# A two-block model kernel on one Trainium2 core: layer 0's modulation rows at another place, and the short convolution's input read from SBUF

## The chip, the cores and the metric

One core of one Trainium2 chip. The metric is device time in microseconds (us) of one execution, smaller is better; PE is TensorE (matrix products), PEld its weight load, DVE is VectorE, ACT ScalarE, POOL GpSimd, SP SyncE, whose queue here issues nearly all loads and stores.

## The reference

A first block (a Hyena long convolution and an HGRN2 scan side by side as mixer, then a mixture of 16 experts that pick their tokens) is followed by a second block of two layers of attention with Fourier and pooling branches. The parts that the change touches:

```python
def short_conv(u, w, b, n_rows):          # first block, width 3, along grid rows of 64
    up = jnp.pad(u.reshape(bn, n_rows, row_len, C), ((0, 0), (0, 0), (pad, pad), (0, 0)))
    y = b + sum(up[:, :, j:j + row_len] * w[j] for j in range(HY_SHORT))

def hyena_mixer(p, n_rows, conv_w, conv_b, filt, bias):
    u = short_conv(p, conv_w, conv_b, n_rows)
    v, x1, x2 = jnp.split(u, 3, axis=-1)
    z = x1 * long_conv(v, hf[:, 0], bias[0])
    y = x2 * long_conv(z, hf[:, 1], bias[1])

def second_block(x, c, ctx, c_ctx, norm_g, w_mod, b_mod, ...):
    for l in range(DEPTH_2):              # 2 layers
        x, ctx = mixer_layer(l, x, ctx, c, c_ctx, norm_g[l], w_mod[l], b_mod[l], ...)
```

Each layer of the second block scales, shifts and gates its input by modulation vectors silu(c) @ w_mod[l] + b_mod[l], for the tokens and, from c_ctx, for the context: 1024 x 3072 weights a layer. The first block has its own (ada_w, 1024 x 6144). x is 1024 tokens of 1024 values, the context 256 tokens, all float32.

## The kernel before

The program runs in stages. 0 to about 110 us: constants, the first two of six column groups of the first block's modulation, normed tokens. To 776.5 us, the **Hyena stage**: the long convolution's filters, spectra and products (`filter_time`, `filter_spectra`, `hyena`) beside the projections of the tokens (`hy_proj`, `hg_proj`) and beside `mods_layer(0, ...)`, the second block's modulation for layer 0. To 1041 us, the **HGRN scans**: `ctx_state` and four times `hgrn_head`, with small work of the first block's remaining modulation (`mods_tail`) and of the second block's context (`ctx_first`, `ctx_side`) woven in. To about 1203 us, **out_proj** and the routing. Then the experts, to about 2600 us, and the two attention layers.

Each engine runs its instructions in one fixed order. The program is written as streams; `side_by_side` (lines 1979 to 1990) weighs those of the Hyena stage against one another, and a scheduler, which sees the whole program, then sets the order on each engine by the rings of buffers that are open (`K.open`, with the count of each ring) and its own estimate of times. PE works in order, and `self.dma` (line 160) puts every load and store on SP's one queue.

Names and lines that matter here:
- `mod_rows` (290 to 313) makes 1024 modulation columns for both c and c_ctx. There are eight **k-steps**: the load of 128 x 1024 weights (512 KB), and two matmuls (L193) that hold the weights as the moving operand and the two silu columns as the stationary one, 2 x 512 each. Then come two bias loads, four adds on DVE (L171), two stores. The whole of `mods_layer` (333 to 343) is three such groups, 24 k-steps, then `rows_to_cols` (315), which reads the rows back and transposes them, and two instructions that make the scale A. `mods_tail` (345) is four groups, 32 k-steps.
- `hy_proj` (789 to 832): for each of 12 channel tiles and 2 token halves, `proj` (421) makes 128 x 512 of projection in a PSUM buffer `pp` (three of them) by 24 matmuls (L188 to L190). The short convolution (821 to 828) is one ACT instruction (scale and bias, middle tap) into a `u2` buffer `u`, and two DVE instructions (L180) that add the left and right tap, all three reading `pp`. `turn` transposes the previous result, copies it out (L168) and stores it.
- `run` (1993): pools at 1996 to 2004, `side_by_side` at 2007 to 2009, the scans' extra work at 2022 to 2030 (PSUM buffers `cp` and `cm`, one each; weight rings `wr` of two and `mr` of one).
- `ctx_first` transposes the normed context (`cp<-ident,cx`), applies layer 0's scale and shift (`cu`, and `Tc`, its two split halves), and projects it: the matmuls `cp<-Tc,wh` and `cp<-Tc,wl`, in blocks of 24. `ctx_side` makes its side branches and its gate by more such blocks. They need layer 0's modulation.

```python
side_by_side((30, 450, [(K.filter_time(), 2.4), (K.filter_spectra(), 2.1), (K.hyena(), 5)]),
           (0, 64, [(K.hy_proj(), 1), (K.hg_proj(), 1)]),
           (0, 4, [(K.mods_layer(0, "mp", "u2", ("mr",), False), 1)]))
```

Of the kernel before, what the change touches and what calls it, by code (L numbers as in the profile page):

```python
# [14 lines left out]
AF = mybir.ActivationFunctionType  # L15
# [99 lines left out]
class Work:  # L115
# [673 lines left out]
    def hy_proj(self):  # L789

        I = self.I
        w = I["w_in"][0]
        ocw, ocb = self.offs["hy_conv_w"], self.offs["hy_conv_b"]
        self.dhy = self.dram([3, 2, 2, 128, 4, 256], name="dhy")
        cw2 = self.cst([128, 4, 4], name="cw2")

        def turn(u, dst):
            pt = self.ps("pp", [128, 4, 128])
            for a in range(4):
                self.tr(pt[:, a], u[:, a * 128:a * 128 + 128])  # L800
            ut = self.t("u2", [128, 4, 128])
            self.cp(ut, pt)
            self.dma(dst, ut)

        late = None
        for g in range(3):
            if g == 2:
                yield from self.hg_values()
                for j in range(3):
                    self.tt(cw2[:, j], self.ca[:, ocw + j * 12 + 8:ocw + j * 12 + 12], self.finv, MUL)  # L810
                self.tt(cw2[:, 3], self.ca[:, ocb + 8:ocb + 12], self.finv, MUL)
            for half in range(2):
                for ct in range(2):
                    c = g * 4 + half * 2 + ct
                    wp = self.wunits(w, c * 128, 128, self.nc.gpsimd)
                    if g == 2:
                        cw = [cw2[:, j, c - 8:c - 7] for j in range(4)]
                    else:
                        cw = [self.ca[:, ocw + j * 12 + c:ocw + j * 12 + c + 1] for j in range(3)] + [self.ca[:, ocb + c:ocb + c + 1]]
                    for th in range(2):  # L820
                        ps = self.proj(wp, self.hT, th * 512, 512, "pp")
                        u = self.t("u2")
                        self.act(u, ps, AF.Identity, scale=cw[1], bias=cw[3])
                        pv = ps.rearrange("p (r c) -> p r c", c=64)
                        uv = u.rearrange("p (r c) -> p r c", c=64)
                        self.stt(uv[:, :, 1:], pv[:, :, :63], cw[0], uv[:, :, 1:], MUL, ADD)
                        self.stt(uv[:, :, :63], pv[:, :, 1:], cw[2], uv[:, :, :63], MUL, ADD)
                        if late:
                            turn(*late)
                        late = (u, self.dhy[g, half, th][:, :, ct * 128:ct * 128 + 128])  # L830
                        yield
        turn(*late)
# [1146 lines left out]
def side_by_side(*streams):  # L1979

    todo = [[-lead / total, total, list(gens)] for lead, total, gens in streams]
    while todo:
        s = min(todo, key=lambda t: t[0])
        g, w = s[2][0]
        if next(g, todo) is todo:
            s[2].pop(0)
            if not s[2]:
                todo.remove(s)
        else:
            s[0] += w / s[1]  # L1990


def run(K):
    fst = ExitStack()
    with ExitStack() as e1:
        K.open(e1, "left", ar=3, ah=4, al=4)
        K.open_ps(e1, "left", pp=3, mp=1)
        K.open(e1, "left", u2=4, T=16)
        K.open_ps(fst, "right", pf=4)
        K.open(fst, "right", f4=7, fb=5)  # L2000
        with ExitStack() as e2:
            K.open(e2, "right", cr=6, x=4, c=2, mr=4)
            K.start()
        K.open(fst, "right", y=3, t=4, H=2, hs=3, dc=2, ri=7, ra=2, mr=1)
        K.load_dft()
        K.mods_first()
        side_by_side((30, 450, [(K.filter_time(), 2.4), (K.filter_spectra(), 2.1), (K.hyena(), 5)]),
                   (0, 64, [(K.hy_proj(), 1), (K.hg_proj(), 1)]),
                   (0, 4, [(K.mods_layer(0, "mp", "u2", ("mr",), False), 1)]))
    fst.close()  # L2010
    with ExitStack() as cx:
        with ExitStack() as e1:
            K.open_ps(e1, "left", ph0=3, ph1=3)
            K.open(e1, "left", hmk=1, hS=2)
            for p in "01":
                K.open(e1, "left", **{"hi" + p: 6, "hw" + p: 5, "h2" + p: 3, "hm" + p: 4, "hT1" + p: 2, "hT2" + p: 4})
            K.ctx_state()
            for h in range(4):
                K.hgrn_head(h)
            K.open(cx, "right", wr=2, wh=2, wl=2, cu=6, cv=2, Tc=4, lg=2)  # L2020
            K.pfx = "c"
            with ExitStack() as e2:
                K.open_ps(e2, "right", cp=1, cm=1)
                K.open(e2, "right", mr=1)
                for _ in K.mods_tail("cm", "cv", ("wr", "wr", "mr"), False):
                    pass
                K.ctx_first()
                K.ctx_side()
                for _ in K.mods_layer(1, "cm", "cv", ("wr", "wr", "mr"), False):
                    pass  # L2030
        K.open_ps(cx, "right", cp=1, cm=1)
        K.pfx = "o"
        em = cx.enter_context(ExitStack())
        with ExitStack() as e0:
            K.open_ps(e0, "left", pp=3, pq=2, pi=1)
            with ExitStack() as e1:
                K.open(e1, "left", xm=3, rw=1, wo=16, m4=3, yt=6, u2=3)
                K.out_proj()
            K.open(em, "left", el=4, eh=4, er=10)
            with ExitStack() as e1:  # L2040
                K.open(e1, "left", twr=3, twh=3, twl=3)
                K.open(e1, "left", aff=1, tk=12, tp=2, af=4)
                K.topk()
                K.pfx = "c"
                K.ctx_heads("tw")
        with ExitStack() as e1:
            K.open_ps(e1, "left", et=1, ea=3, ey=2)
            K.open(e1, "right", g2b=1, xg=1, xf=1, xh=4, sa=4, hh=4, yo=2)
            side_by_side((0, 64, [(K.moe(), 1)]), (CL, CT, [(K.ctx_rest(), 1)]))
    K.pfx = ""  # L2050
    with ExitStack() as e1, ExitStack() as e0, ExitStack() as ec:
        K.open(e0, "right", T0=16)
        rope = K.lat_pools(ec)
        hT = K.first_rows()
        K.lat_path(hT, rope, ec, e0, e1)


class Kern:
# [9 lines left out]
    def start(self):  # L2068
        W = self.work
        W.pc, W.psm, W.pd, W.one = self.pc, self.psm, self.pd, self.one  # L2070
        run(W)
# [119 lines left out]
```

## Time and profile before

| what | value |
|---|---|
| median of 3 runs (lowest, highest) | 3840.05 us (3839.73, 3846.28) |
| the profiled execution's own time | 3841.8 us |
| its span, first to last instruction | 3839.7 us |
| mean granted TensorE clock | 0.963 of 2.4 GHz |
| PE, DVE, ACT, POOL busy | 92%, 71%, 58%, 29% of the span |
| DMA | 780.49 MB, mean 203 GB/s |

The shares are means over stages with different limits; the table of stretches below tells them apart. A row of that table gives, for one stretch of the span, the busy time of each engine with its number of instructions, the granted clock as a share of full speed, and the busy share and rate of the DMA engines. A row on a group of instructions gives line, engine, operation, output and inputs (buffer numbers left out), shape and number; then busy time, mean duration in ns, and the idle time of the engine ahead of them with what ended it. A matmul of float32 with 512 columns shows as two records.

### The profile page before, as it was taken

The page shows a single profiled execution, that of the slowest core. Times are in us where ns is not written, and L with a number is a line of the kernel's source. Part 1 is how long each engine was busy: PE and PEld are TensorE (multiplying, and loading weights), DVE is VectorE, ACT ScalarE, POOL GpSimd, SP SyncE. Part 2 cuts the span into 40 slices and gives each one's busy share as a digit, 9 for nine tenths or more (in the row PEclk, how much of TensorE's full clock was granted, in tenths as well). Part 3 has the DMA queues.
Part 4 walks back from the last instruction along what each step waited for, and adds up shares of the span by engine and source line. Part 5 has one row for each costly group of instructions (what it writes and reads, how often), then busy time and mean ns, then how long its engine had stood idle before and what let it go on. Part 6 is the DMA issues. An engine that isn't in the chain of part 4 may idle for free. (4 is left out here: it accounts for less than half of the span.)

```text
span 3839.7 us, 50939 instructions
## 1 busy us (share of the span) xinstructions
PE 3533.6 (92%) x17554; PEld 2841.9 (74%) x17554; DVE 2727.8 (71%) x4143; ACT 2219.1 (58%) x3568; POOL 1127.8 (29%) x702
## 2 busy tenths in 40 slices
PE   5998999968897799999999999979999899999989
PEld 2666878747867678787777777768777688877767
DVE  3488667777735789889889889866666744576672
ACT  4432322354525786787777777755576754456762
POOL 2355423364414214112112111001333610133361
PEclk9999999979998899999999999989999999999999
DMA  6765444464476699999999999952311144131133
GB/s 206 220 222 181 130 145 128 141 211 147 132 246 218 200 341 347 336 333 364 371 366 358 370 367 357 364 185 81 128 60 43 47 155 132 59 128 54 39 104 115
DMA packets 503019, 780.49 MB, mean 203 GB/s; under 512 B 35025, under 2 KB 238823, under 8 KB 502504
## 3 DMA queue, kind: packets, MB, share of 16 engines
q1 hardware_dynamic: 496136, 755.74, 57.8%
q0 software_dynamic: 5600, 20.43, 2.0%
q8 instruction: 138, 2.26, 0.2%
q10 hardware_dynamic: 1024, 1.06, 0.1%
q14 instruction: 121, 0.99, 0.1%
HBM read 669.00 MB, written 107.05 MB: 202 GB/s over the span
## 5 line engine op out<-in xcount | busy, mean ns | idle before, releaser
L171 DVE TENSOR_TENSOR el<-er,eh 128x1024 fp32r<-128x1024 f32 x763 | 950.7, 1296 | 107.9 <-ACT eh L168 105.8
L168 ACT ACTIVATE eh<-er 128x1024 fp32r<-128x1024 f32 x768 | 782.4, 1057 | 116.1 <-PE ea L190 83.5
L189 PE MATMUL ea<-el,xh 128*128 128x512 f32 x1024 | 413.9, 404 | 21.0 <-DVE el L171 18.1
L188 PE MATMUL ea<-eh,xh 128*128 128x512 f32 x1024 | 399.2, 393 | 2.4 <-ACT eh L168 2.2
L190 PE MATMUL ea<-eh,xh 128*128 128x512 f32 x1024 | 401.1, 392 | 0.0
L1265 POOL DMA_INDIRECT acc<-yo,idx x16 | 74.0, 4626 | 808.8 <-DVE yo L180 754.9
L1488 DVE TENSOR_SCALAR_CACHE_REDUCE E<-s,rq 128x512 f32<-128x512 f32 (+1 forms) x384 | 237.2, 656 | 80.8 <-PE s L193 70.0
L189 PEld LDWEIGHTS ea<-el,xh 128*128 128x128 f32 x1024 | 192.6, 188 | 94.1 <-DVE el L171 58.4
L165 ACT ACTIVATE E<-E,a 128x1280 f32<-128x1280 f32 x160 | 216.7, 1359 | 66.5 <-DVE a L1492 61.5
L193 PE MATMUL s<-KA,QA 128*128 128x512 f32 (+1 forms) x768 | 212.6, 398 | 32.1 <-DVE E L1488 31.1
L188 PEld LDWEIGHTS ea<-eh,xh 128*128 128x128 f32 x1024 | 192.5, 188 | 46.4 <-ACT eh L168 4.2
L190 PEld LDWEIGHTS ea<-eh,xh 128*128 128x128 f32 x1024 | 193.0, 189 | 34.3 <-POOL xh L171 0.3
L189 PE MATMUL ey<-el,hh 128*128 128x512 f32 x512 | 203.8, 398 | 6.2 <-DVE el L171 6.2
L188 PE MATMUL ey<-eh,hh 128*128 128x512 f32 x512 | 202.0, 399 | 2.1 <-ACT eh L168 2.1
L190 PE MATMUL ey<-eh,hh 128*128 128x512 f32 x512 | 200.3, 391 | 0.0
L171 POOL TENSOR_TENSOR wl<-wr,wh 128x1024 fp32r<-128x1024 f32 (+1 forms) x48 | 116.6, 2434 | 253.7 <-ACT wh L168 193.3
L193 PEld LDWEIGHTS s<-KA,QA 128*128 128x128 f32 x768 | 131.4, 199 | 78.8 <-DVE E L1488 60.3
L168 ACT ACTIVATE u<-pp 32x512 f32<-32x512 f32 (+2 forms) x212 | 124.4, 587 | 106.3 <-PE pp L190 85.6
L193 PE MATMUL po<-th,V 128*128 128x256 f32 x640 | 172.5, 395 | 13.7 <-ACT th L168 13.6
L188 PE MATMUL pp<-T,ah 128*128 128x512 f32 x448 | 183.0, 408 | 1.6 <-ACT ah L168 1.6
L190 PE MATMUL pp<-T,al 128*128 128x512 f32 x448 | 179.2, 400 | 0.4 <-POOL al L171 0.4
L189 PE MATMUL pp<-T,ah 128*128 128x512 f32 x448 | 178.7, 399 | 0.0
(516 smaller groups left out, 8944.2 us busy)
## 6 DMA issues: line engine op xcount, KB each, us to landing
er<-in_exp_w_dram SPq DMA_DIRECT2D x768, 512.0 KB
wr<-in_w_in_dram SPq DMA_DIRECT2D x60, 512.0 KB
ar<-in_w_in_dram SPq DMA_DIRECT2D x64, 256.0 KB
mr<-in_w_mod_dram SPq DMA_DIRECT2D x30, 512.0 KB
wr<-in_ada_w_dram SPq DMA_DIRECT2D x24, 512.0 KB
wr<-in_w_out_dram SPq DMA_DIRECT2D x24, 512.0 KB
Hd<-hs SPq DMA_DIRECT2D x72, 128.0 KB
H<-Hd SPq DMA_DIRECT2D x36, 256.0 KB
```

The costliest lines, as they stand in the source:

```text
L165: return self.nc.scalar.activation(out, in_, func, **kw)
L168: return self.nc.scalar.activation(out, in_, AF.Copy)
L171: return (eng or self.nc.vector).tensor_tensor(out, a, b, op=op)
L188: mm(out, lh, rh, start=first, stop=False)
L189: mm(out, lh, rl, start=False, stop=False)
L190: mm(out, ll, rh, start=False, stop=last)
L193: self.nc.tensor.matmul(out, l, r, start=first, stop=last)
L1265: nc.gpsimd.indirect_dma_start(out=self.acc, out_offset=x[0], in_=yo, in_offset=None, compute_op=ADD)
L1488: nc.vector.tensor_scalar(E[:, k0:k1], o, r, None, op0=MUL, op1=ALU.min, accum_out=mx[:, m, j:j + 1] if nc_ > 1 else mc)
```

## The change

Three edits. (a) In the short convolution, a new ACT copy brings the projection from PSUM into a `u2` buffer `raw`; the ACT instruction and both DVE instructions then read `raw`. That is 24 copies. (b) `mods_layer(0, ...)` leaves the Hyena stage and is issued in the scans' block, ahead of `mods_tail`, with the PSUM buffer `cm`, the temporary `cv` and the weight ring of two `wr` and one `mr`. (c) Rings: u2 from 4 to 5 buffers, t from 4 to 5, cr from 6 to 5, and the `mr` buffer of the Hyena stage goes. The PSUM buffer `mp` stays.

```diff
--- before.py
+++ after.py
@@ -819,9 +819,11 @@
                         cw = [self.ca[:, ocw + j * 12 + c:ocw + j * 12 + c + 1] for j in range(3)] + [self.ca[:, ocb + c:ocb + c + 1]]
                     for th in range(2):
                         ps = self.proj(wp, self.hT, th * 512, 512, "pp")
+                        raw = self.t("u2")
+                        self.cp(raw, ps)
                         u = self.t("u2")
-                        self.act(u, ps, AF.Identity, scale=cw[1], bias=cw[3])
-                        pv = ps.rearrange("p (r c) -> p r c", c=64)
+                        self.act(u, raw, AF.Identity, scale=cw[1], bias=cw[3])
+                        pv = raw.rearrange("p (r c) -> p r c", c=64)
                         uv = u.rearrange("p (r c) -> p r c", c=64)
                         self.stt(uv[:, :, 1:], pv[:, :, :63], cw[0], uv[:, :, 1:], MUL, ADD)
                         self.stt(uv[:, :, :63], pv[:, :, 1:], cw[2], uv[:, :, :63], MUL, ADD)
@@ -1995,18 +1997,17 @@
     with ExitStack() as e1:
         K.open(e1, "left", ar=3, ah=4, al=4)
         K.open_ps(e1, "left", pp=3, mp=1)
-        K.open(e1, "left", u2=4, T=16)
+        K.open(e1, "left", u2=5, T=16)
         K.open_ps(fst, "right", pf=4)
         K.open(fst, "right", f4=7, fb=5)
         with ExitStack() as e2:
-            K.open(e2, "right", cr=6, x=4, c=2, mr=4)
+            K.open(e2, "right", cr=5, x=4, c=2, mr=4)
             K.start()
-        K.open(fst, "right", y=3, t=4, H=2, hs=3, dc=2, ri=7, ra=2, mr=1)
+        K.open(fst, "right", y=3, t=5, H=2, hs=3, dc=2, ri=7, ra=2)
         K.load_dft()
         K.mods_first()
         side_by_side((30, 450, [(K.filter_time(), 2.4), (K.filter_spectra(), 2.1), (K.hyena(), 5)]),
-                   (0, 64, [(K.hy_proj(), 1), (K.hg_proj(), 1)]),
-                   (0, 4, [(K.mods_layer(0, "mp", "u2", ("mr",), False), 1)]))
+                   (0, 64, [(K.hy_proj(), 1), (K.hg_proj(), 1)]))
     fst.close()
     with ExitStack() as cx:
         with ExitStack() as e1:
@@ -2022,6 +2023,8 @@
             with ExitStack() as e2:
                 K.open_ps(e2, "right", cp=1, cm=1)
                 K.open(e2, "right", mr=1)
+                for _ in K.mods_layer(0, "cm", "cv", ("wr", "wr", "mr"), False):
+                    pass
                 for _ in K.mods_tail("cm", "cv", ("wr", "wr", "mr"), False):
                     pass
                 K.ctx_first()
```

Where the instructions stand, as each engine has them in order. In these rows a name is a tile with its buffer numbers, and x2 means two in a row.

ACT in the Hyena stage, at the first token halves of `hy_proj`, before (`u_347_1189` is a convolution's result, `pp_1164` the projection in PSUM, `ah` a split weight, `fb` and `t` the filters' work):

```order
L165 ACTIVATE fb_948<-t_957 128x512
L165 ACTIVATE u_347_1189<-pp_1164,cols_129 128x512
L165 ACTIVATE t_972<-t_968 128x512
L168 ACTIVATE ah_1572<-ar_1570 128x512
L168 ACTIVATE ah_1578<-ar_1576 128x512
L165 ACTIVATE u_372_1300<-pp_1275,cols_129 128x512
```

and with the change (`u_346_1186` is `raw`):

```order
L165 ACTIVATE fb_945<-t_954 128x512
L168 ACTIVATE u_346_1186<-pp_1161 128x512
L165 ACTIVATE t_969<-t_965 128x512
L165 ACTIVATE u_347_1188<-u_346_1186,cols_129 128x512
L168 ACTIVATE ah_1534<-ar_1532 128x512
L168 ACTIVATE ah_1540<-ar_1538 128x512
```

The copy stands where the convolution's ACT instruction stood, and that one comes one or two places later, with other work between them at times.

PE at the start of the scans, just behind the last projection of `hg_proj`, before (`cm_8090` are k-steps of mods_tail with the first block's `silu_118`, `cp` the context's transposes, `ph` the scans' own work):

```order
L190 MATMUL pp_6229<-T_345,al_6197 128x512
L193 MATMUL cm_8090<-wr_8091,silu_118 2x512 x2
L193 MATMUL cm_8090<-wr_8095,silu_118 2x512 x2
L193 MATMUL cm_8090<-mr_8099,silu_118 2x512 x2
L196 MATMUL cp_8354<-ident_107,cx_8333 128x128
L196 MATMUL cp_8354<-ident_107,cx_8335 128x128
L196 MATMUL cp_8361<-ident_107,cx_8333 128x128
L196 MATMUL cp_8361<-ident_107,cx_8335 128x128
```

and with the change (`silu_930` is the second block's, so `cm_7995` are k-steps of layer 0):

```order
L190 MATMUL pp_6135<-T_345,al_6103 128x512
L193 MATMUL cm_7995<-wr_7996,silu_930 2x512 x2
L193 MATMUL cm_7995<-wr_8000,silu_930 2x512 x2
L193 MATMUL cm_7995<-mr_8004,silu_930 2x512 x2
L196 MATMUL cp_8398<-ident_107,cx_8377 128x128
L196 MATMUL cp_8398<-ident_107,cx_8379 128x128
L196 MATMUL ph_1557_6373<-ident_107,hw_1548_6324 128x128 x2
L193 MATMUL cm_7995<-wr_8008,silu_930 2x512 x2
L193 MATMUL ph_1559_6378<-hw_1524_6233,h_1558_6376 128x128 x2
L196 MATMUL ph_1560_6382<-ident_107,hw_1548_6324 128x128 x2
```

Layer 0's k-steps take the places that mods_tail's first ones had, woven between the scans' matmuls; the context's other 14 transposes come only behind them, and mods_tail's 32 k-steps behind these.

PE at the end of the scans and the start of out_proj, before (`pi` is the router's first transpose and belongs to out_proj, `pp<-wo,yt` is out_proj's product, `cp<-Tc,wh` a context block of 24 matmuls):

```order
L190 MATMUL cp_8873<-Tc_8330,wl_8870 128x256
L196 MATMUL pi_9204<-ident_107,m_2265_9200 128x128 x4
L193 MATMUL cm_8935<-wr_8936,silu_933 2x512 x2
L188 MATMUL pp_9261<-wo_9130,yt_9182 128x512
L189 MATMUL pp_9261<-wo_9131,yt_9182 128x512
```

and with the change:

```order
L193 MATMUL ph_1956_7958<-ident_107,ss_7954 128x128 x4
L193 MATMUL cp_8641<-k2b_8480,fz_8608 128x256 x4
L196 MATMUL pi_9234<-ident_107,m_2285_9230 128x128 x4
L188 MATMUL cp_8657<-Tc_8373,wh_8650 128x256
L189 MATMUL cp_8657<-Tc_8375,wh_8650 128x256
```

Of the 288 context matmuls `cp<-Tc` 216 stood ahead of the scans' end and 72 behind it; now 72 stand ahead and 216 behind, which moves 144, six blocks of 24, into out_proj.

## Rows read from the trace of the kernel before

**Rows 1.** The page, its head.

```profile
span 3839.7 us, 50939 instructions
```

**Rows 2.** Busy time of each engine by stretch.

```profile
core 0: us, PE busy (x) PEld busy (x) DVE busy (x) ACT busy (x) POOL busy (x), PEclk, DMA share, GB/s
110.00:776.50 666.50, 624.83 (x2895) 496.25 (x2891) 482.31 (x792) 204.93 (x437) 280.02 (x188) 0.97 0.52 165
250.00:375.00 125.00, 104.73 (x511) 80.80 (x510) 106.69 (x160) 35.28 (x90) 67.25 (x41) 0.89 0.57 185
776.50:832.00 55.50, 30.75 (x150) 13.35 (x148) 40.08 (x90) 21.33 (x50) 31.34 (x40) 0.74 0.75 252
832.00:892.00 60.00, 54.17 (x369) 40.53 (x370) 55.75 (x88) 40.18 (x112) 37.60 (x27) 0.90 0.48 166
892.00:936.00 44.00, 36.49 (x245) 31.17 (x244) 23.07 (x47) 14.85 (x30) 14.91 (x8) 0.84 0.61 188
936.00:1041.00 105.00, 89.92 (x715) 87.08 (x714) 83.95 (x127) 56.96 (x146) 62.60 (x44) 0.93 0.29 87
1041.00:1203.00 162.00, 150.47 (x778) 109.82 (x777) 59.38 (x98) 66.31 (x149) 33.02 (x22) 0.96 0.71 240
1041.00:1052.00 11.00, 7.39 (x59) 6.67 (x60) 9.76 (x10) 5.83 (x10) 4.61 (x2) 1.00 0.97 296
```

**Rows 3.** Timeline of PE: start, duration; a k-step and the next instruction.

```profile
490.47 1.03 PE L193 MATMUL mp<-mr,silu 128*2 128x512 f32 x4
491.43 0.92 PE L193 MATMUL pf<-y,dc 128*128 128x256 f32 x3
```

**Rows 4.** Tile mp alone by stretch: PE, PEld, DVE, ACT busy.

```profile
110.00:776.50 666.50, 28.66 (x97) 2.59 (x93) 8.17 (x12) 0.18 (x1) 0.97 0.52 165
250.00:375.00 125.00, 9.22 (x28) 0.81 (x28) 2.72 (x4) 0.00 (x0) 0.89 0.57 185
```

**Rows 5.** Groups of ACT, Hyena stage: copies out of `pp`.

```profile
L168 ACT ACTIVATE u<-pp 128x512 f32<-128x512 f32 x32 | 18.9, 592 | 16.3 <-PE pp L196 8.8 <-PE pp L190 5.3 <-DMA dhy<-u 2.1
```

**Rows 6.** Waits of DVE, Hyena stage: total us, times, longest.

```profile
DVE u L180 <- ACT u L165: 23.3, 10, 5.9
```

**Rows 7.** Waits of PE, Hyena stage.

```profile
PE pp L196 <- DVE u L180: 4.0, 2, 2.4
```

**Rows 8.** Groups of DVE, Hyena stage: the convolution (cols, cw), the nearest SBUF form.

```profile
L180 DVE SCALAR_TENSOR_TENSOR u<-pp,cols,u 128x504 f32<-128x504 f32 x32 | 23.4, 734 | 6.3 <-ACT u L165 6.0
L180 DVE SCALAR_TENSOR_TENSOR u<-pp,cw,u 128x504 f32<-128x504 f32 x16 | 11.8, 739 | 17.4 <-ACT u L165 17.3
L180 DVE SCALAR_TENSOR_TENSOR y<-fb,f 128x512 f32<-128x512 f32 x12 | 8.2, 680 | 1.5 <-PE pf L193 1.4
```

**Rows 9.** Issues of cr loads on SP: ns (min/median/max), first and last start.

```profile
L161 SPq DMA_DIRECT2D cr<-in_w_in_dram x24: 367/385/1734, 19.2 to 119.1; - x24
```

**Rows 10.** Tile cm alone, start of the scans: PE, PEld, DVE, ACT busy.

```profile
776.50:892.00 115.50, 27.24 (x108) 2.64 (x108) 8.14 (x12) 0.00 (x0) 0.82 0.61 207
```

**Rows 11.** Waits of PE's weight load, scans.

```profile
PEld cm L193 <- DMA wr<-in_ada_w_dram: 2.6, 3, 1.2
```

**Rows 12.** Groups of DVE, scans: the context's modulation and split.

```profile
L171 DVE TENSOR_TENSOR Tc<-cu,Tc 128x256 fp32r<-128x256 f32 x8 | 4.3, 540 | 0.3 <-ACT Tc L168 0.3
L177 DVE TENSOR_SCALAR cu<-cp,A,mods 128x256 f32<-128x256 f32 x4 | 2.1, 537 | 2.8 <-PE cp L196 2.8
```

**Rows 13.** Timeline of PE: two matmuls of a context block.

```profile
1038.06 0.28 PE L189 MATMUL cp<-Tc,wh 128*128 128x256 f32 x1
1038.18 0.28 PE L190 MATMUL cp<-Tc,wl 128*128 128x256 f32 x1
```

**Rows 14.** Timeline at the start of the scans: DVE and POOL adds.

```profile
780.57 0.41 DVE L171 TENSOR_TENSOR Tc<-cu,Tc 128x256 fp32r<-128x256 f32 x1
...
783.17 1.54 POOL L171 TENSOR_TENSOR hw<-hw,hw 128x128 f32<-128x128 f32 x2 [20.01 <-DVE hw L177]
...
783.60 0.73 DVE L171 TENSOR_TENSOR Tc<-cu,Tc 128x256 fp32r<-128x256 f32 x1
```

## The prediction

> **What bounds the kernel now.** I read the page's head first, for the span [rows 1]: 3839.7 us, with 2.1 us around it in the profiled execution's 3841.8 us. The median of the three runs is 3840.05 us, so the sum below is made against 3841.8 us and then taken from the median, 1.75 us lower. About 0.2%, here 7.7 us, is what a measurement of this kernel can tell from no change.
>
> Next I read busy time by stretch [rows 2], since the change takes work from one stretch and gives it to later ones. The reader is to see that the busiest engine changes from row to row.
> - 110 to 776.5 us, the Hyena stage: TensorE (PE) is busy 624.8 of 666.5 us. But inside it, from 250 to 375 us, VectorE (DVE) is busy 106.7 of 125 us and PE leaves 20.3 us idle.
> - 776.5 to 832 us, start of the HGRN scans: PE 30.8 of 55.5, DVE 40.1. From 832 to 892 us DVE 55.8 of 60.
> - 892 to 936 us: PE 36.5 of 44, no engine full. From 936 to 1041 us: PE 89.9 of 105, DVE 84.0.
> - 1041 to 1203 us, out_proj and routing: PE 150.5 of 162. This is the stretch most nearly bound by PE alone.
>
> So a PE microsecond taken out is worth nearly one in the Hyena stage, little at the start of the scans, and costs nearly one in out_proj. The change moves PE work through all three.
>
> **The change, part by part.**
>
> *Moved: the 24 k-steps of layer 0's modulation rows.* One k-step is a PE entry of four records that holds PE for 491.43 − 490.47 = 0.96 us [rows 3]. The tile `mp` has 97 PE records in the Hyena stage [rows 4]: 24 k-steps of four and one transpose. Removing them takes 24 × 0.96 = 23.0 us from PE. But 28 of the records, 7 k-steps or 6.7 us, lie between 250 and 375 us, where DVE sets the pace [rows 2, 4]. There only the 4 adds come back, 2.72 us of DVE [rows 4], so 4.0 us of the 23.0 are not recovered: −19.0. The one 0.18 us copy on ScalarE (ACT) that goes with it [rows 4] lies beside an engine busy for 205 of 666.5 us [rows 2]: zero.
>
> *Added: the copy in the convolution.* 24 ACT copies of 128x512; the same shape out of the same PSUM pool takes 592 ns [rows 5], so 14.2 us on an engine with 461 us idle there [rows 2]. Off the path unless DVE waits for them: DVE works in order, and its two conv instructions wait for the ACT instruction ahead of them, which now stands behind another. Before, ten of these waits cost DVE 23.3 us [rows 6], and behind the waiting conv stand the filter products that PE waits for. Ten waits, each 0.59 us longer, would be 5.9 us; all 24 would be 14.2. The other way, the PSUM buffer comes free after the copy rather than after two DVE instructions: PE's transposes into `pp` waited 4.0 us for them [rows 7]. Bounds −4.0 to +14.2; I take half of the 5.9, +3, because only some of those waits stand in the DVE-bound stretch. The two DVE instructions now read on-chip memory (SBUF) alone: 734 and 739 ns now, against 680 ns for the nearest form without PSUM [rows 8], so 48 × 0.055 = 2.6 us of DVE, which I leave in the range. If cover on ACT went, the +14.2 would be due.
>
> Hyena stage: −19.0 + 3 = −16 (bounds: −23.0 − 4.0 = −27, and −19.0 + 14.2 = −4.8).
>
> *Pools.* The rings u2 and t grow by one, cr shrinks by one, mr=1 goes. The cr loads at the start are 24 issues from 19.2 to 119.1 us [rows 9], one in 4.3 us on average; a load that comes one place later costs between 0 and that. I take 0: no wait of PE for such a load is named in the trace there.
>
> *Start of the scans, 776.5 to 892 us.* The 24 k-steps take the places that 27 of mods_tail's 32 had (108 records [rows 10]); PE there gets 3 k-steps less, under DVE: zero. Their 12 adds stand for the same kind of adds. On SP's queue 24 weight loads, 6 bias loads, 6 stores and 2 read-backs, 38 issues, now stand ahead of mods_tail's; the POOL queue gets none. DMA is busy 75% there at 252 GB/s [rows 2], and the same ring of three weight buffers fed 27 k-steps with only 2.6 us of waits, three in number [rows 11]. So I cost the loads at zero; the cover is that DVE, not PE, is late. What leaves is the context block's modulation: by the order its transposes now come where 893 us is today, and with them 4.3 + 2.1 = 6.4 us of DVE [rows 12]. These stood at 780 to 799 us, where DVE's chain leads to the first scans. Bounds −6.4 to 0; I take −5, since little DVE idle lay inside the 20 us.
>
> *892 to 936 us.* By the order 16 of mods_tail's 32 k-steps stand here instead of the 5 that are left after the first 27 [rows 10]: 11 × 0.96 = +10.6, while 24 context matmuls leave, 24 × 0.12 = −2.9 (spacing of one, [rows 13]). Net +7.7 against 7.5 us of PE idle [rows 2]. Idle of a chain can't all be filled; bounds 0 to +7.7, I take +3, nearer the idle being used.
>
> *936 to 1041 us.* 120 context matmuls leave, −14.4; 16 k-steps of mods_tail come, +15.4. Zero, with 15 us of PE idle as cover [rows 2]; if that is not usable, +1.
>
> *Out_proj.* The 144 context matmuls, six blocks of 24, come here: 144 × 0.12 = +17.3 us of PE [rows 13], where PE is the bound. From 1041 to 1052 us PE is idle 11 − 7.4 = 3.6 us [rows 2], where the first block fits: +13.7. Bounds +10 (the 162 − 150.5 = 11.5 us of idle taken up for two thirds) and +17.3.
>
> **Sum:** −16 − 5 + 3 + 0 + 13.7 = −4.3 us: 3837.5 against the profiled execution, **3835.8 against the median, say 3836**. With all bounds at their ends: −27 − 6.4 + 0 + 10 = −23.4, or −4.8 + 4.3 + 0 + 7.7 + 1 + 17.3 = +25.5. The forecast's own range is 3826 to 3848. So 23 us of PE work leave one stage and come back, mostly, two stages later, as other work that has been pushed out.
>
> **A rule of the Trainium skill that speaks against the copy.** What the row shows: DVE adds with two SBUF inputs of 128x256 take 0.41 us beside no GpSimd (POOL) work and 0.73 us where a POOL instruction overlaps [rows 14], 0.32 us or 78% more. The Trainium skill, "SBUF — State Buffer", section "Who interferes with whom", says that a DVE instruction with two SBUF inputs contends with a GpSimd instruction that reads SBUF, and that one with at most one SBUF input does not; the trace agrees with the first half by these two durations. By that rule the 48 conv instructions, which until now took one input from PSUM, become exposed; this is rival 3. The Trainium skill, "VectorE: DVE Perf Modes", section "Rules for kernel authors", advises copying out of PSUM "if you'll do many ops"; here three instructions read it, and by that advice the gain would be no more than the 2.6 us above.
>
> **Rivals.**
>
> *1. All PE time comes back (0.20).* The stage before is PE-bound throughout, the freed PSUM bank pays for the copy, the DVE start gains in full, and out_proj absorbs the blocks at the lower bound: −23.0 − 6.4 + 0 + 10 = −19.4, 3821 us. For it: PE busy 94% of the stage. Against: the 20.3 us idle from 250 to 375 us [rows 2].
>
> *2. Slower: the k-steps wait for their weights (0.15).* In the scans PE takes its instructions in order, and the k-steps stand between the scans' own transposes; a late weight holds the scan behind it. Before, a wait cost 2.6 / 3 = 0.87 us [rows 11]. If each of the 24 waits so, +21, and the start gains nothing: −16 + 21 + 13.7 = +18.7, 3859 us. It decides once the stretch from 776.5 to 1041 us grows by 10 us or more. For it: 12.6 MB more in a stretch that begins with DMA 75% busy. Against: mods_tail's 27 k-steps in the same places waited three times only.
>
> *3. The conv instructions contend with POOL (0.12).* POOL is busy 280 of 666.5 us, 42% [rows 2]. If 42% of 48 instructions, 20, grow by 78% of 0.73 us, 0.57 each, DVE gets +11.5 us; all on the path at worst: −4.3 + 11.5 = +7.2, 3847 us. Against: DVE is idle 184 us in that stage.
>
> *4. The change moves work and time is conserved (0.08).* What leaves the first stage comes back in full: 0, 3840 us.
>
> **How the numbers follow.** The forecast has 0.45. Within its own range it gives 0.17 faster by over 7.7 us (below 3832.4), 0.235 within, 0.045 slower (above 3847.7). Rival 1 adds 0.20 faster; rival 2 adds 0.15 slower; rival 3, at the edge, 0.06 within and 0.06 slower; rival 4 adds 0.08 within. Together 0.37 faster, 0.375 within, 0.255 slower; rounded 0.37, 0.38, 0.25. The range reaches from 3818, which takes in rival 1 with some spread, to 3854: outside it are most of rival 2 and the outer ends of the bounds, not more than 0.2. Most chance lies on both signs, so the forecast's own range, 3826 to 3848, is the narrower statement.
>
> **What would show it.** Right: the Hyena stage, from the first filter matmul to the last projection, 16 us shorter with 24 `mp` k-steps gone; DVE's conv waits for ACT somewhat longer than 23.3 us; the scans about as long as before; out_proj some 14 us longer with 216 context matmuls in it; everything after 1203 us unchanged but shifted by −4 us. The copy is wrongly priced if conv instructions of DVE read over 0.8 us each (rival 3) or if the stage shrinks by less than 5 us. The placing is wrongly priced if PE waits for `wr` or `mr` loads by over 10 us between 776 and 1041 us (rival 2). It is wrong as a whole if out_proj is not longer: then the 144 matmuls found idle PE, and rival 1's time or a lower one is due. A difference after 1203 us above 3 us would be outside every case here.

## The result, and the profile after

The changed kernel is slower, by 0.5 to 0.6%: 3866.61 us median of four runs (3854.16 to 3869.49) against 3839.89 us, ratio 1.0061 with a 95% interval of 1.0043 to 1.0078. In a second set of five runs it took 3861.48 us against 3841.39 us, ratio 1.0047 (1.0033 to 1.0061). The forecast was 3836 us; both medians lie above its range. The first profiled execution was the fastest of its four, 3854.2 us, the second (3868.7 us) the slowest of its five; both are used below, since they bracket the medians.

The head of the page, for [rows 1]:

```profile
span 3852.4 us, 50937 instructions
```

Busy time by stretch, for [rows 2], with the borders where the same events now stand: the last projection, the last matmul of the scans, the router's last, the experts' first and last. Columns as there.

```profile
110.00:767.10 657.10, 598.19 (x2792) 498.99 (x2794) 482.71 (x775) 215.70 (x455) 281.10 (x188) 0.96 0.47 149
767.10:1028.50 261.40, 209.70 (x1416) 153.41 (x1416) 207.06 (x362) 126.45 (x323) 130.58 (x108) 0.90 0.59 193
1028.50:1205.40 176.90, 167.03 (x932) 128.17 (x930) 60.07 (x99) 73.99 (x163) 49.48 (x29) 0.97 0.71 236
1205.40:1283.60 78.20, 50.37 (x344) 45.70 (x343) 62.96 (x103) 36.18 (x82) 43.22 (x29) 0.76 0.65 186
1283.60:2512.40 1228.80, 1188.21 (x5479) 954.98 (x5479) 1084.45 (x1029) 945.95 (x1135) 207.72 (x78) 1.00 0.99 348
```

The kernel before has these borders at 776.8, 1041.0, 1202.5, 1286.2 and 2507.0 us. The last three of its stretches:

```profile
1041.00:1202.50 161.50, 150.43 (x778) 109.82 (x777) 58.99 (x96) 66.31 (x149) 32.64 (x21) 0.96 0.71 239
1202.50:1286.20 83.70, 52.72 (x346) 47.26 (x345) 66.88 (x108) 37.18 (x85) 42.77 (x29) 0.74 0.62 175
1286.20:2507.00 1220.80, 1188.76 (x5476) 954.51 (x5476) 1078.68 (x1022) 946.91 (x1134) 206.95 (x78) 1.00 0.99 350
```

The Hyena stage ends 9.7 us earlier, not 16. The scans shorten by 264.2 − 261.4 = 2.8 us, out_proj lengthens by 15.4 us: both near the forecast (2 and 13.7). So the routing ends at 1205.4 us, 2.9 us later than before. Behind it the top-k search with the context's heads takes 5.5 us less, the experts' stretch 8.0 us more, and the two attention layers behind the experts 1340.0 us (to the span's end) rather than 1332.7, 7.3 us more: 9.8 us in sum, which was in no case of the prediction. In the second profiled execution the Hyena stage ends only 3.0 us earlier and the routing 13.6 us later, with 1228.9 us for the experts and 1344.2 us for the attention layers.

The DVE instructions of the convolution in the changed kernel, for [rows 8], first as groups (busy, mean ns), then with the shortest, median and longest of one in ns:

```profile
L180 DVE SCALAR_TENSOR_TENSOR u<-u,cols,u 128x504 f32<-128x504 f32 x32 | 33.4, 1044 | 4.5 <-ACT u L165 4.2
L180 DVE SCALAR_TENSOR_TENSOR u<-u,cw,u 128x504 f32<-128x504 f32 x16 | 13.1, 821 | 15.9 <-ACT u L165 15.8
```

```profile
L180 DVE SCALAR_TENSOR_TENSOR u<-u,cols,u x32: 680/742/2278, 144.2 to 299.8; 128x504 f32<-128x504 f32 x32
L180 DVE SCALAR_TENSOR_TENSOR u<-u,cw,u x16: 729/742/1202, 409.1 to 479.8; 128x504 f32<-128x504 f32 x16
```

Before, the mean was 734 and 739 ns. Now the median is still 742 ns, but 16 of the 48 take 1.15 to 2.28 us, and the 48 together 46.5 us rather than 35.2.

### The profile page after: what moved, and what is told of

Same layout as the page of the kernel before. It is cut to its first block, busy times and chain, and to the rows that moved or that the text cites. A ratio compares the mean times of both kernels' runs of the same rounds, so it can differ in the third digit from the quotient of the medians.

```text
span 3852.4 us, 50937 instructions
## 1 busy us (share of the span) xinstructions
PE 3519.8 (91%) x17554; PEld 2845.6 (74%) x17554; DVE 2739.5 (71%) x4143; ACT 2231.3 (58%) x3590; POOL 1132.5 (29%) x702
## 5 line engine op out<-in xcount | busy, mean ns | idle before, releaser
L168 ACT ACTIVATE u<-pp 32x512 f32<-32x512 f32 (+2 forms) x236 | 138.3, 586 | 116.6 <-PE pp L190 96.1
```

The lines of the kernel that those rows point to most:

```text
L168: return self.nc.scalar.activation(out, in_, AF.Copy)
```

## The experiments

The theories: A, the move makes the loss; B, the copy makes it; C, any edit makes the scheduler put the context's work and the experts in another order, and the loss is made there; D, within B, that the convolution's DVE instructions, with both inputs in SBUF, contend with POOL; E, within B, that the copy delays ACT's instruction.

### The changed kernel again, the two edits apart, and a ring alone

The first is the kernel as it is; the second has only the copy (the first hunk of the diff), with the rings of before; the third only the move, with the rings of the change (the other hunks); the fourth is a control:

```diff
-            K.open(e2, "right", cr=6, x=4, c=2, mr=4)
+            K.open(e2, "right", cr=5, x=4, c=2, mr=4)
```

The change again: 

> The changed kernel once more, unaltered, for a second profile and a narrower interval. Its first profiled execution took 3854.2 us while three timed ones took 3865.8 to 3869.5. If the 12 us between them are a matter of the executions (theory: one stretch behind the routing runs in two ways), this profile shows 3854 or about 3867, and in the latter case one stretch holds the further 12 us. If the difference is drift of the chip, times spread evenly between 3850 and 3870.

The copy alone: 

> Only the copy out of PSUM, rings as before, modulation rows where they were. Theory A (the move makes the loss, the copy is hidden on ScalarE): within 4 us of the kernel before, 3836 to 3844. Theory B (the copy makes the loss: the convolution waits and contends with POOL): 3855 to 3870, with the Hyena stage 10 us or more longer. Theory C (any edit changes the scheduler's order of the context's layer beside the experts, and the loss is made there): the Hyena stage moves by under 4 us, and the experts' stretch from 1284 to 2512 us by 3 to 10 us either way.

The move alone: 

> Only the move, with the rings of the change; the convolution reads PSUM as before. Theory A: 3854 to 3868, as the changed kernel. Theory B: 3825 to 3840, no slower than before. Theory C: somewhere between 3835 and 3870, with the stretches up to 1203 us as in the changed kernel within 4 us and the difference behind them.

One cr buffer fewer: 

> The kernel before with one buffer fewer in the ring cr (5 for 6), which alone should cost 0 to 4 us in the first 130 us. Theories A and B: 3838 to 3845, and everything behind 130 us as before, shifted as a whole. Theory C: the time behind the routing changes by 3 us or more, though nothing there was edited.

Measured, against 3841.39 us: the change 3861.48, the copy alone **3859.17** (ratio 1.0047, 1.0033 to 1.0061), the move alone **3842.89** (1.0007, 0.9998 to 1.0016), cr=5 alone 3850.38 (1.0031, 1.0019 to 1.0044). The changed kernel's times spread from 3854 to 3869 us. Of the 14.6 us between its two profiles 6.7 lie in the Hyena stage, 4.2 behind the experts and the rest in smaller parts, so no one stretch holds them. Theory A falls: with these rings the move costs next to nothing, the copy about as much as both. Theory B's forecast holds for the copy (3855 to 3870) and is missed by 3 us for the move (3825 to 3840). The copy alone, Hyena stage and the DVE instructions:

```profile
110.00:788.90 678.90, 629.09 (x2899) 503.49 (x2899) 497.88 (x792) 218.61 (x460) 284.07 (x188) 0.95 0.51 162
```

```profile
L180 DVE SCALAR_TENSOR_TENSOR u<-u,cols,u x32: 721/744/2277, 147.7 to 306.1; 128x504 f32<-128x504 f32 x32
L180 DVE SCALAR_TENSOR_TENSOR u<-u,cw,u x16: 729/744/1202, 421.9 to 492.3; 128x504 f32<-128x504 f32 x16
```

The stage ends at 788.9 us, 12.1 us later; the experts' stretch is as before (1297.7 to 2518.7 us, 1221.0), and what lies behind it takes 6.0 us more (1338.7 us). The move alone, from the Hyena stage to the experts:

```profile
110.00:757.00 647.00, 597.85 (x2788) 498.65 (x2792) 478.05 (x775) 200.45 (x427) 277.38 (x186) 0.96 0.47 151
757.00:1018.50 261.50, 210.59 (x1416) 154.70 (x1416) 207.72 (x362) 126.71 (x323) 127.97 (x108) 0.90 0.59 193
1018.50:1195.60 177.10, 166.84 (x931) 128.17 (x930) 59.69 (x99) 74.14 (x163) 49.46 (x29) 0.97 0.70 236
1195.60:1272.40 76.80, 50.27 (x344) 45.73 (x343) 63.23 (x103) 36.27 (x82) 43.27 (x29) 0.77 0.66 190
1272.40:2502.90 1230.50, 1189.66 (x5479) 956.67 (x5479) 1084.18 (x1028) 945.82 (x1135) 207.25 (x78) 0.99 0.99 348
```

Here the Hyena stage is 19.8 us shorter, the scans 2.7 us, out_proj 15.6 us longer: the routing ends 6.9 us earlier. The top-k stretch takes 6.9 us less as well, the experts 9.7 us more, so that they still end 4.1 us earlier; the attention layers then take 5.5 us more (1338.2 us). So the move is carried out as the prediction had it up to the routing, and eaten behind it.

### Is it the source of the DVE instructions, or the copy itself?

The kernel with the copy alone, the ACT instruction reading the copy, and only this undone:

```diff
-                        pv = raw.rearrange("p (r c) -> p r c", c=64)
+                        pv = ps.rearrange("p (r c) -> p r c", c=64)
```

> The kernel before with the copy, where the ACT instruction reads the copy but the two DVE instructions read PSUM as before. With the copy alone those DVE instructions grew from 734 to 1061 ns (the 32 with cols) and the Hyena stage by 12 us. Theory D (they grow because with two SBUF inputs they contend with POOL, and that growth is on the path): back at 734 ns, Hyena stage within 4 us of before, 3838 to 3847. Theory E (the copy delays ACT's instruction, and DVE's order with it): still 3853 to 3864 and the stage 8 us or more longer, though the DVE instructions are back at 734 ns.

Measured: **3846.77 us** against 3842.82 (ratio 1.0009, 0.9999 to 1.0018), 12.4 us less than the copy alone with the DVE instructions on SBUF. The stage and the instructions:

```profile
110.00:775.10 665.10, 622.70 (x2889) 497.44 (x2893) 477.96 (x791) 217.69 (x459) 275.50 (x188) 0.97 0.53 165
```

```profile
L180 DVE SCALAR_TENSOR_TENSOR u<-pp,cols,u x32: 679/733/744, 147.3 to 301.9; 128x504 f32<-128x504 f32 x32
L180 DVE SCALAR_TENSOR_TENSOR u<-pp,cw,u x16: 727/731/744, 412.6 to 482.0; 128x504 f32<-128x504 f32 x16
```

The stage ends at 775.1 us, 13.8 us ahead of the copy alone, and none of these DVE instructions is longer than 744 ns. Both kernels do the same copies on ACT, so theory E falls and D's forecast holds. But the input of 48 DVE instructions is not all that differs: the scheduler put the work of the two in another order, with 2088 of PE's 17554 instructions in other places. The same one-line edit on the whole change has no such flaw:

> The whole change, but the two DVE instructions of the convolution read PSUM again (ACT's reads the copy). Theory D (with two SBUF inputs they lose time to POOL, 11 us of DVE, all on the path): 3843 to 3851, the Hyena stage 10 us or more shorter than in the changed kernel's profiles and its end near 757 us. If the loss of the whole change is the move's work behind the stage: 3855 to 3867.

Measured: 3853.54 us against 3842.15 (1.0033, 1.0021 to 1.0045), the stage's end at 762.5 us. It is 8 us below the changed kernel's second median and 13 below its first, and between the two forecasts, which were both missed. In the traces all four engines run the same instructions in the same order as in the second profile of the changed kernel, from the first to the last, so here only the input of 48 DVE instructions differs. The Hyena stage in this run, then in that second profile:

```profile
110.00:762.50 652.50, 601.96 (x2792) 500.90 (x2796) 473.43 (x776) 215.53 (x455) 274.80 (x188) 0.96 0.47 150
110.00:773.80 663.80, 604.82 (x2790) 503.31 (x2794) 483.87 (x775) 214.58 (x454) 279.95 (x186) 0.95 0.46 147
```

The stage's end alone would say 11.3 us here and 4.6 us against the first profile. The 6.7 us between these two profiles are PE's own busy time, 604.8 against 598.2 us in two executions of one kernel, at a granted clock of 0.95 and 0.96 of 2.4 GHz. The time in which PE is idle (length less busy time) is steadier: 59.0 and 58.9 us in the changed kernel, 50.5 with DVE on PSUM, 49.2 with the move alone; and without the move 49.8 with the copy alone, 42.4 with DVE on PSUM, 41.7 in the kernel before. So the SBUF input costs PE 7.4 to 8.4 us of waiting, the copy on ACT 0.7 and 1.4 us. The experts' stretch keeps the move's lengthening (1230.7 us).

That POOL is what holds the DVE instructions is seen in single ones. The copy alone, timelines of POOL and of DVE near 306 us (start, duration):

```profile
305.29 2.52 POOL L171 TENSOR_TENSOR f<-f,f 128x768 f32<-128x768 f32 x1
```

```profile
303.03 3.12 DVE L171 TENSOR_TENSOR f<-f,f 128x768 f32<-128x768 f32 x1
306.08 2.28 DVE L180 SCALAR_TENSOR_TENSOR u<-u,cols,u 128x504 f32<-128x504 f32 x1
```

POOL's add runs to 307.81 us; the DVE instruction starts at 306.08 and ends 0.55 us after it. Over that trace, 23 of the 48 overlap no work of POOL and take 0.737 us on average; 25 do, and take 1.209. In the trace of before, with one input in PSUM, 29 that overlap none and 19 that do both take 0.736 us. What counts is who was first: 18 of the 48 start while an add of POOL runs, and among them are all 16 that take over 0.8 us; the other 32 take at most 0.745. Each of the 16 ends 0.54 to 0.55 us after the end of that add, and the same holds for the 16 long ones in each profile of the changed kernel. Before, 17 started during an add of POOL, and none took over 0.744 us. The Trainium skill, "SBUF — State Buffer", section "Who interferes with whom", says that a DVE instruction with two SBUF inputs contends with a POOL instruction that reads SBUF, that the order of issue decides which of the two is blocked, and that a DVE instruction with at most one SBUF input does not contend outside what it calls the 2-port perf modes; these means and starts agree. Alone, reading SBUF instead of PSUM saves nothing: 0.737 against 0.736 us.

### What the move costs behind the scans, and the rings

The move alone, with the rings of the kernel before:

```diff
-        K.open(e1, "left", u2=5, T=16)
+        K.open(e1, "left", u2=4, T=16)
-            K.open(e2, "right", cr=5, x=4, c=2, mr=4)
+            K.open(e2, "right", cr=6, x=4, c=2, mr=4)
-        K.open(fst, "right", y=3, t=5, H=2, hs=3, dc=2, ri=7, ra=2)
+        K.open(fst, "right", y=3, t=4, H=2, hs=3, dc=2, ri=7, ra=2)
```

> Only the move, with the rings u2, t and cr of the kernel before (4, 4, 6). 262 context matmuls stand in out_proj rather than 216. If the rings are worth nothing: 3843 plus 46 x 0.12 = 5.5 us, 3844 to 3852. If cr=5 costs what the kernel with cr=5 alone showed as its median (+9 us): 3834 to 3843.

Measured: 3866.25 us against 3842.82 (1.0057, 1.0043 to 1.0071), a miss. Out_proj takes 190.1 us with 262 context matmuls in it, where 46 more should have cost 5.5 us and cost 13, and the experts 1234.7 us. Three ring sizes in an early stage thus decide 23 us in the median, all of it behind the scans; beyond the 46 matmuls it is not shown what costs it. The control again:

> The kernel with cr=5 once more. Its profile stood 1.2 us above the one of before, but the median of six runs 9 us above. If that is a matter of executions that differ in one stretch, this profile falls anywhere from 3842 to 3860 and shows the stretch; if cr=5 costs the ctx projection's loads, the profile shows the first 130 us longer by up to 9 us.

Measured: 3850.93 us against 3842.82 (1.0020, 1.0011 to 1.0029), the same 8 to 9 us as the first time. Its Hyena stage is not longer (end at 775.4 us against 776.8). One row for what lies behind the experts, in the control's two profiles and in the kernel before (in this order, one from each):

```profile
2504.00:3840.90 1336.90, 1233.21 (x6272) 1020.11 (x6272) 802.63 (x1709) 775.65 (x1315) 388.96 (x221) 0.97 0.29 94
```

```profile
2505.40:3848.60 1343.20, 1235.12 (x6273) 1022.38 (x6272) 804.74 (x1709) 776.18 (x1315) 387.70 (x221) 0.96 0.29 93
```

```profile
2507.00:3839.60 1332.60, 1238.65 (x6272) 1021.90 (x6272) 804.04 (x1709) 776.70 (x1315) 389.64 (x221) 0.96 0.29 94
```

The control takes 4 and 11 us more there, in a part that the edit doesn't name; its order differs from that of before until 3460 us on POOL and 3715 to 3723 us on the other engines. So an edit that should do nothing costs 8 us, as theory C has it. That the order is the cause isn't shown: these two profiles have one order and differ by 6.3 us there, and the thirteen profiles other than the one of before have 1336.0 to 1344.2 us there, though some differ from before in few places.

Could the room in out_proj be won? Layer 1's modulation rows, 24 k-steps there, put elsewhere:

```diff
-                for _ in K.mods_layer(1, "cm", "cv", ("wr", "wr", "mr"), False):
-                    pass
...
                 K.ctx_heads("tw")
+                for _ in K.mods_layer(1, "cp", "cv", ("wr", "twr"), False):
+                    pass
```

With the move: 

> Only the move, and layer 1's modulation rows taken out of out_proj as well and put behind the context's heads beside the top-k search (PE idle 29 of 81 us there in the run with the move only). If out_proj is bound by PE, as its lengthening by 15.7 us in the run with the move only says, it shrinks by about 24 x 0.96 = 23 us, and the time falls to 3820 to 3832. If the experts' stretch behind it, bound by DMA and DVE, swallows it (12.6 MB more ahead of the experts' weights, some 35 us of DMA at 360 GB/s): 3838 to 3855.

The same lines ahead of the context's heads, with the move: 

> The move, with layer 1's modulation rows run between the top-k search and the context's heads, so ahead of the heads, and not behind them. Behind them, their k-steps ran from 1236 to 1292 us and the experts' stretch grew by 22 us. If those late loads were what delayed the experts: routing ends near 1173 us, experts start 15 to 28 us ahead of the kernel before and keep at least 10 of it, 3822 to 3835. If the experts give it back for another cause (order of the context's layer beside them): 3838 to 3850.

There, without the move: 

> The kernel before with only layer 1's modulation rows put there, layer 0's left in the Hyena stage. If out_proj is bound by PE: routing ends 15 to 23 us earlier than 1202.5 us; the context's work is then as in the kernel before, so the experts' stretch should stay near 1221 us from the first to the last matmul, and the time is 3818 to 3832. If the top-k stretch swallows the k-steps only in part: 3832 to 3842.

And the context's gate projection taken to behind the heads (the loop over `gate_steps` at the end of `ctx_side` goes, the same loop stands behind `ctx_heads`), with the move: 

> The move alone, with the context's gate projection (eight blocks of 24 matmuls) taken out of the stretch before the routing and issued behind the context's heads, where PE is idle 25 to 30 us beside the top-k search. Of the 264 context matmuls behind the routing 96 then stand ahead of the first expert matmul, 72 more among the experts. If out_proj's lengthening by 15.7 us in the run with the move only was these blocks: routing ends 15 to 23 us ahead of the kernel before. If the experts' stretch, 1220 to 1221 us where layer 0's rows stay and 1229 to 1231 us where they move, is lengthened by context work that arrives late: it grows further, to 1235 us or more, and the time is 3838 to 3852. If it isn't: 3822 to 3835.

Measured: 3845.03 us (ratio 1.0011, 1.0002 to 1.0020), 3864.23 (1.0063, 1.0049 to 1.0076), 3869.72 (1.0068, 1.0055 to 1.0082) and 3838.44 (0.9995, 0.9985 to 1.0004). The routing does end early, at 1172.8, 1170.1, 1179.6 and 1174.4 us, 23 to 32 us ahead of before, as a PE-bound out_proj demands. But ahead of the heads the k-steps hold up the top-k stretch: 115.8 and 113.9 us rather than 83.7, and both runs miss every time forecast for them, by 14 us and more. And the experts' stretch grows in each of the four. Its rows, for k-steps late, ahead of the heads with and without the move, and gates late, one from each:

```profile
1256.90:2499.40 1242.50, 1199.53 (x5537) 958.82 (x5537) 1093.43 (x1052) 954.14 (x1150) 215.76 (x82) 0.99 0.99 350
```

```profile
1285.90:2519.20 1233.30, 1193.82 (x5488) 960.78 (x5488) 1086.39 (x1046) 957.32 (x1156) 205.51 (x82) 0.99 0.99 347
```

```profile
1293.50:2527.30 1233.80, 1194.15 (x5488) 960.87 (x5488) 1086.59 (x1046) 957.18 (x1156) 205.86 (x82) 0.99 0.99 347
```

```profile
1255.50:2493.10 1237.60, 1197.71 (x5560) 964.38 (x5560) 1090.75 (x1048) 961.42 (x1166) 218.05 (x86) 1.00 0.99 349
```

The length goes up with the work of DVE in it: 1078.1 to 1079.2 us of DVE and 1220.2 to 1221.0 us in the five profiles with both layers' rows where they were; 1084.2 to 1084.5 and 1228.8 to 1230.7 in the four with the move and the change's rings; 1086.4 and 1086.6 with 1233.3 and 1233.8; 1089.5 with 1234.7; 1090.8 with 1237.6; 1093.4 with 1242.5. The changed kernel has seven more DVE instructions there than before; six are steps of the context's attention, which stood ahead of the first expert. PE's waits in the experts' stretch, before and after:

```profile
PE ea L189 <- DVE el L171: 18.1, 18, 1.5
```

```profile
PE ea L189 <- DVE el L171: 24.1, 24, 2.0
```

6.0 of the 8 us are waits for `el`, the experts' weights that DVE splits. The top-k stretch ahead of it lost 5.5 us, so part of the 8 us may be time that only changed its place. No run took only these steps out of the stretch, so this cause is argued from fourteen profiles, not isolated. No version beat the kernel before clearly: the gates late are 3 us below it, with an interval that holds no change.

## Why the prediction was wrong

**The k-steps out of the Hyena stage: right.** −19.0 forecast, −19.8 in the move alone.

**The scans and out_proj: right.** −2 and +13.7 forecast, −2.7 and +15.6 measured. Rival 2 (late weights) came only in small. Waits of PE's weight load for layer 0's weights and for mods_tail's, which are now issued behind them, for [rows 11], in the changed kernel:

```profile
PEld cm L193 <- DMA wr<-in_w_mod_dram: 0.6, 1, 0.6
PEld cm L193 <- DMA wr<-in_ada_w_dram: 7.1, 3, 4.1
```

The second was 2.6 us before. It stays below the 10 us that the prediction gave as the sign, and the scans grew shorter.

**The copy: mis-sized, and this step made most of the loss.** The prediction said that the "two DVE instructions now read on-chip memory (SBUF) alone" and would gain 2.6 us, which it left in the range, and put the copy at +3 us. They lost 46.5 − 35.2 = 11.3 us (47.2 − 35.2 = 12.0 with the copy alone), and the Hyena stage became 9.7 and 3.0 us shorter, not 16. The copy put 12.1 us on the stage's end alone, 10.1 and 16.8 us with the move; 7.4 to 8.4 us of this are PE's waiting for the contention with POOL. The sign that the prediction had named came: the groups read 1044 and 821 ns, over 0.8 us. This is rival 3. Its price of +11.5 us came out right by luck: it had 20 instructions longer by 0.57 us, and 16 grew by 0.71. The argument against it, 184 us of idle DVE in the stage, was a mean over the stage and does not protect an engine that waits for single results. Nor is the loss confined to where DVE sets the pace, 250 to 375 us in [rows 2]. Against the run of the same order with DVE on PSUM, the projections of the changed kernel are 3.7 and 8.2 us behind at 229 us of that run, 6.0 and 8.7 us at 250 us, and 7.2 and 11.2 us at 431 us (first and second profile). There, from 150 to 250 us, PE is busy 91.7 and DVE 85.8 of 100 us: neither is full.

**A row read wrongly.** The prediction took the 4.0 us of [rows 7] as PE waiting for a PSUM buffer that the copy would free. L196 is the transpose that reads `u`: whatever buffer it writes, it waits for the convolution's result, so a buffer that is free earlier had nothing to win there. The same wait in the changed kernel, with the copy alone, and with the copy and DVE on PSUM:

```profile
PE pp L196 <- DVE u L180: 10.0, 4, 4.4
PE pp L196 <- DVE u L180: 4.8, 3, 2.5
PE pp L196 <- DVE u L180: 9.0, 5, 4.0
```

It doesn't follow the loss: it is small where the stage grew by 12.1 us, and large where the stage did not grow. The waits of DVE for ACT in [rows 6], from which the +3 us came, were forecast to grow from 23.3 us and fell to 20.0. ACT's part of the copy puts 5.5 us on the stage's end with the move (762.5 against 757.0 us) and none without it (775.1 against 776.8); all but 1.4 of the 5.5 us are PE's busy time, which differs by more between two executions of one kernel.

**"Everything after 1203 us unchanged but shifted": wrong.** This term was put at nothing. It measured +9.8 and +13.7 us in the changed kernel's two profiles and +8.3 us in the move alone, against the one profile of before: less in the top-k stretch, more in the experts, where context steps that had been pushed back now lie, and 5.5 to 11.5 us more in the attention layers. For the last the cause stays open; the control shows 4 and 11 us at the same place.

**The width.** The 7.7 us taken for what a measurement can tell apart is less than what an idle edit costs: 8 to 9 us for one cr buffer, whose cost was put at 0, with 4.3 as its end.

Together: in medians the copy alone cost 17.8 us, the move alone 1.5, both 20.1 in the same set of runs. The first profile lies 17.0 us above the forecast's sum: 6.3 of them in the Hyena stage, 9.8 behind the routing. In the second it is 31.6 us, 13.0 and 13.7 at these places. Rival 3's 3847 us was too low because it, too, had nothing behind the routing. What is shown is the contention, 8 to 13 us in medians; of the rest, part is PE's busy time and part lies behind the routing, where no run isolates it.

## What to carry to other kernels

Moving an input of a two-input DVE instruction from PSUM to SBUF is not free where POOL is busy: price it by the share of time that POOL runs beside it, and do not discount the price by the idle time of DVE over a stage, since an engine that works in order waits for single results. Work taken out of one PE-bound stage comes back where it pushes other work, so follow what it displaces to the end of the program. Where a scheduler orders the whole program, measure an idle edit as a control before crediting an edit with less than that, and before isolating a cause look whether the two kernels compared have the same order.

## What was not expected of the hardware

A DVE instruction of 0.73 us can take 2.28 us when it starts 0.8 us into a POOL add of 2.52 us: it ends 0.55 us after it. So do all 48 long ones of three traces, 0.54 to 0.55 us after the POOL add in which they started, though one that is not held takes 0.73 us: by these numbers about 0.2 us of an instruction is not held up (an estimate). Those of the convolution that start before the POOL add are not held at all (at most 0.746 us). And the same instruction is not faster from SBUF than from PSUM where nothing disturbs it (0.737 and 0.736 us).
